# Memory keys of layer 0 as single fp32 products, memory norms kept for layer 1, and a scheduler with other durations

## The chip, the cores and the metric

One core of a Trainium2 chip runs the kernel. The time is device microseconds of one execution, the median of three runs: 822.15 us (821.66 to 822.86). TensorE (PE in the profile; its weight loads are PEld) multiplies, VectorE (DVE), ScalarE (ACT) and GpSimd (POOL) work element by element, SyncE (SP) issues all DMAs from one queue in order.

## What is computed

Two layers of a decoder trunk over 256 tokens of width 1024. Layer 0 mixes tokens by a gated delta rule (GDN), layer 1 by sparse attention (NSA). Both layers also attend to 256 memory tokens with 4 heads, and both normalise the same memory, each with its own weight vector:

```python
def rms_norm(x, w):
    y = x * lax.rsqrt(jnp.mean(x * x, axis=-1, keepdims=True) + EPS)
    return y * w

def memory_attention(qm, mem_n, w_kv):
    kv = (mem_n @ w_kv).reshape(B, -1, 2, MEM_HEADS, HEAD_DIM)
    k, v = kv[:, :, 0], kv[:, :, 1]
    s = jnp.einsum('bshd,bmhd->bhsm', qm, k) * HEAD_DIM ** -0.5
    return jnp.einsum('bhsm,bmhd->bshd', jax.nn.softmax(s, axis=-1), v)

for i in range(2):
    h = rms_norm(x, norm_mix_w[i])
    mem_n = rms_norm(mem, mem_norm_w[i])
    proj = h @ (gdn_w_in, nsa_w_in)[i]       # the last 512 columns are qm
    ...                                      # GDN or NSA on the other columns
    x = x + jnp.concatenate([mix, memory_attention(qm, mem_n, mem_w_kv[i])], -1) @ w_out[i]
    x = x + conv_glu(rms_norm(x, norm_ffn_w[i]), ffn_w_up[i], ...)
return rms_norm(x, final_norm_w)
```

The factor 1/rms of a memory token does not depend on the layer.

## The kernel before

**Products.** All matrices are cut into tiles of 128 by 128 weights against 128 by 256 data. The accuracy of fp32 is kept by splitting each operand into a high part and a rest in the type fp32r: `hi` is a rounded copy (ACT), `lo` is the difference (DVE, or POOL for memory weights). A product is then three fp32r products (`hi*hi`, `hi*lo`, `lo*hi`), in `proj`. Small products (scores, norms, GDN) are plain fp32 instead; the profile records one fp32 product as two matmul records. A weight chunk is loaded (`wr`, `mr`), cast (`wh`, `mh`) and subtracted (`wl`, `ml`) before TensorE uses it.

**The start.** `mem_in` makes `memh` and `meml` from the memory (`mt`) for values and keys, and squares it (`sq`, summed in `sqa`); `rstd_fin` sums the squares over partitions by products with `ones`, takes the power -1/2 on POOL (`rs`) and spreads the result over the partitions by products with the identity (`mx<-ident,rs`). `mem_k` makes one head's keys from 8 blocks of weights (24 products, tile `pf`) and scales them by the norm (`kTm`). The tokens `xall` go through the same norm, become `hn`, then `xh` and `xl`, and the projections `pj` of the GDN layer follow. For layer 1 `mem_in` loads the memory again, squares it by DVE or POOL (`sq_acc`) and takes the norm again.

**What sets the order.** Nothing runs in the order in which it is written. Class `Sched` (line 54) takes all operations, gives each a duration (`_cost`, line 416) and simulates the five engines: at each step the engine that can start earliest takes its next ready operation, buffers counted (`order`). What comes out is the fixed order of each engine's queue. For some operations it also chooses the engine (DVE or POOL). So a changed duration can move instructions anywhere. In the profile all of them carry the line of the helper that issues them, L379, and are told apart by tile names. In the change that line is L380.

**Durations in it.** An fp32r product of 256 columns counted 0.109 us, an fp32 one 0.43 us.

The lines that the change touches first:

```python
            if dt == F32R:
                return 0.0025 + max(2 * m, n) / 2400
            return 0.005 + 4 * max(m, n) / 2400
...
        for t in range(2):
            mm(pb[:, t * P:(t + 1) * P], rs[:, t:t + 1].to_broadcast([P, P]), ident, start=True, stop=True)
...
            xs.append(split(mts[k], V_NMEM + layer * KD + k, "mem", KD))
            if layer:
                acc = sq_acc(acc, mts[k])
            elif k % 2 == 0:
                acc = sq_pair(acc, mts[k].t)
        return (xs,) + rstd_fin(acc, keep="col")
```

Of the kernel before, what the change touches and what calls it, by code (L numbers as in the profile page):

```python
# [10 lines left out]
F32 = mybir.dt.float32  # L11
# [8 lines left out]
P = 128  # L20
# [35 lines left out]
class Sched:  # L56
# [66 lines left out]
    def order(self):  # L123
# [48 lines left out]
        while todo:  # L172
# [46 lines left out]
            if op.dma:  # L219
                hw_t = max(hw_t, st + 0.05) + 0.457  # L220
                dma_t = max(dma_t, hw_t + 0.65) + op.cost
                eng_t[op.eng] = st + 0.06
                op.end = dma_t + 0.75
            else:
                op.end = st + op.cost
                eng_t[op.eng] = op.end
            op.st = st
            out.append(op)
# [154 lines left out]
class Eng:  # L383
# [36 lines left out]
    def _cost(self, m, a, kw, out, e):  # L420
        ins = [x for x in list(a) + list(kw.values()) if isinstance(x, (Vt, Ap)) and x is not out]
        n = max([math.prod(x.shape[1:]) for x in [out] + ins[:2] if isinstance(x, (Vt, Ap))] or [1])
        ps = any((x.t if isinstance(x, Ap) else x).cls == "ps" for x in ins)
        if m == "dma_start":
            sh = out.shape
            return math.prod(sh) * 4 / 360e3
        if e == "tensor":
            n = math.prod(out.shape[1:])
            rhs = a[2]
            if m == "transpose":  # L430
                return 0.11
            dt = (rhs.t if isinstance(rhs, Ap) else rhs).dt
            m = out.shape[0]
            if dt == F32R:
                return 0.0025 + max(2 * m, n) / 2400
            return 0.005 + 4 * max(m, n) / 2400
        if e == "vector":
            if m == "reciprocal":
                return 0.06 + 0.0065 * n
            if m in ("tensor_copy", "tensor_scalar") and not ps:  # L440
                return 0.07 + 0.00055 * n
            return 0.07 + 0.00105 * n + (0.057 if m == "scalar_tensor_tensor" and isinstance(a[2], (Vt, Ap)) else 0.0)
        if e == "scalar":
            ex = sum(isinstance(kw.get(k), (Vt, Ap)) for k in ("bias", "scale")) + ("accum_out" in kw)
            if m == "mul" and isinstance(a[2], (Vt, Ap)):
                ex += 1
            return 0.075 + 0.00085 * n + 0.093 * ex
        if m == "scalar_tensor_tensor" or kw.get("op") == OP.pow and n > 8:
            return 1.0
        if kw.get("op") == OP.pow:  # L450
            return 0.3 + 0.165 * n
        if m == "tensor_scalar":
            return 0.08 + 0.0009 * n if not isinstance(a[2], (Vt, Ap)) else 0.26 + 0.0033 * n
        return 0.14 + 0.00215 * n
# [14 lines left out]
class Weights:  # L469
# [8 lines left out]
    def prep(self):  # L478
        c = self.next
        if c >= self.n:  # L480
            return
        self.next += 1
        sc, ch = self.cx, self.bpc * P
        w = min(ch, self.nblk * P - c * ch)
        raw = sc.tile(self.cls, [P, ch], F32, self.tag + "r", self.bufs)
        sc.t["sync"].dma_start(raw[:, :w], self.src[:, c * ch:c * ch + w])
        hi = sc.tile(self.cls, [P, ch], F32R, self.tag + "h", self.bufs)
        sc.t["scalar"].copy(hi[:, :w], raw[:, :w])
        lo = sc.tile(self.cls, [P, ch], F32R, self.tag + "l", self.bufs)
# [16 lines left out]
def body(ctx, tc, xT, memT, vecs, consts, rows, relb, w_few, w_in0, w_out0, w_up0, w_dn0, w_in1, w_out1, w_up1, w_dn1,  # L506
# [37 lines left out]
    def mx():  # L544
        return sc.tile("ps", [P, 512], F32, "mx", 6)
# [7 lines left out]
    def mm(*a, **kw):  # L553
        PE.matmul(*a, **kw)
# [74 lines left out]
    def sq_pair(acc, src, **kw):  # L629
# [5 lines left out]
            EV.tensor_tensor(out=nacc, in0=nacc, in1=acc, op=OP.add)  # L635
        return nacc

    def rstd_fin(*accs, keep="row"):
        pc = mx()
        for t in range(2):  # L640
            for i, acc in enumerate(accs):
                mm(pc[:, t:t + 1], acc[:, t * P:(t + 1) * P], ones[:, :1], start=i == 0, stop=i == len(accs) - 1)
        ms = Sm("ms", [P, 2])
        V.tensor_scalar(ms, pc[:, :2], 1.0 / D, EPS, op0=OP.mult, op1=OP.add)
        rs = Sm("rs2", [P, 2], 4)
        rsq(rs, ms, 2)
        pb = mx()
        for t in range(2):
            mm(pb[:, t * P:(t + 1) * P], rs[:, t:t + 1].to_broadcast([P, P]), ident, start=True, stop=True)
        if keep == "psum":  # L650
            return pb
        r = K("rs", 2)
        A.copy(r, pb[:, :S])
        return {"row": r, "both": (r, pb), "col": (r, rs)}[keep]
# [19 lines left out]
    def mem_load(k):  # L674
        mt = Dd("mt", 4)
        SY.dma_start(mt, memT[:, k * S:(k + 2) * S])
        return [mt[:, :S], mt[:, S:]]

    def mem_in(layer, mts):
        xs, acc = [], None  # L680
        for k in range(KD):
            xs.append(split(mts[k], V_NMEM + layer * KD + k, "mem", KD))
            if layer:
                acc = sq_acc(acc, mts[k])
            elif k % 2 == 0:
                acc = sq_pair(acc, mts[k].t)
        return (xs,) + rstd_fin(acc, keep="col")

    def mem_k(layer, h, ws, xs, rm):
        ps = proj(ws, h * KD, xs, "pf")  # L690
        kTm[layer, h] = K("kTm", 2 * MH)
        evac(ps, rm, kTm[layer, h])
# [90 lines left out]
        SY.dma_start(xall[:, k:k + 2], xT[:, k * S:(k + 2) * S].rearrange("p (k t) -> p k t", k=2), also_out=x[k:k + 2])  # L783

    wm0 = Weights(sc, w_mem0, 64, "m", 3, ahead=1, cls="d")
    mts = []
    xk = 0
    for ch in "wmmimmwxxxxsb0v":
        if ch == "m":
            mts += mem_load(len(mts))  # L790
        elif ch == "w":
            wm0.prep()
        elif ch == "x":
            x_load(xk)
            xk += 2
        elif ch == "i":
            ident = fixed([P, P], "ident")
            SY.dma_start(ident, consts[:, C_ID:C_ID + P])
        elif ch == "s":
            ms0 = mem_in(0, mts)  # L800
            mem_k(0, 0, wm0, *ms0[:2])
        elif ch == "b":
            wba = few_weights(w_few[:, :16 * KD], 16, "wba")
        elif ch == "0":
            w0.prep()
        elif ch == "v":
            vecb = fixed([P, NV - V_GNORM], "vecb")
            cst = fixed([P, C_HOT - C_TRI], "cst")
            SY.dma_start(cst, consts[:, C_TRI:C_HOT])
            SY.dma_start(vecb, vecs[:, V_GNORM:])  # L810
# [310 lines left out]
    classes["scl"] = classes["scd"] = 2  # L1121
    classes["gsc"] = 1
    pools["scl"] = pools["scd"] = pools["gsc"] = pools["dram"]
    for h in range(1, MH):
        mem_k(0, h, wm0, *ms0[:2])
    prs = [gdn_pair(p) for p in range(H // 2)]
    dh = 0
# [362 lines left out]
```

## Time and profile before

| what | value |
|---|---|
| median of three runs | 822.15 us |
| the profiled execution, its own time | 824.31 us |
| its span | 822.5 us |
| PE busy | 799.3 us (97%), 6645 records |
| DVE busy | 603.2 us (73%) |
| ACT busy | 480.1 us (58%) |
| POOL busy | 169.1 us (21%) |

A busy share is an average over stages. The first 230 us (memory, GDN) are different from the rest, where TensorE runs long lists of equal products. A matmul's duration overlaps the next one's, so the rate is read from the distance between starts. "What ended the idle time" names the last thing waited for.

### The profile page before, as it was taken

What the parts mean: (1) busy time and instruction counts of PE and PEld (TensorE: products, weight loads), DVE (VectorE), ACT (ScalarE), POOL (GpSimd) and SP (SyncE); (2) the same over time, 40 slices, a digit from 0 to 9 for tenths busy, and PEclk for the clock granted to TensorE, in tenths of its full rate; (3) what the DMA queues carried; (4) which work ended last, traced back from release to release, by engine and by line L of the source; (5) the groups of instructions that cost most, each with busy time, mean ns of one, the idle gap of its engine ahead of it and who ended that gap; (6) DMA issues with size and microseconds to landing.
All of it is one profiled execution on the core that took longest, in us unless ns stands there. A gap on an engine that the chain in (4) does not pass through costs nothing.

```text
span 822.5 us, 17100 instructions
## 1 busy us (share of the span) xinstructions
PE 799.3 (97%) x6645; PEld 784.5 (95%) x6645; DVE 603.2 (73%) x1243; ACT 480.1 (58%) x995; POOL 169.1 (21%) x273
## 2 busy tenths in 40 slices
PE   6999899999999999999999999999999999999996
PEld 5999889999999999999999999999999999999995
DVE  6999888887757576776765686798686867776552
ACT  6578475667644655555543466699845555664340
POOL 3267544544110211211101020000010211121000
PEclk9999999999999999999999999999999999999998
DMA  8674435443467456656666558522365656666641
GB/s 316 209 242 142 128 112 159 113 118 110 126 208 217 144 170 190 184 176 185 184 196 183 177 158 291 150 90 67 95 201 157 205 173 177 194 180 179 195 133 52
DMA packets 52926, 137.55 MB, mean 167 GB/s; under 512 B 11572, under 2 KB 17773, under 8 KB 52717
## 3 DMA queue, kind: packets, MB, share of 16 engines
q1 hardware_dynamic: 52844, 136.46, 54.8%
q8 instruction: 52, 0.85, 0.4%
q14 instruction: 30, 0.24, 0.1%
HBM read 134.06 MB, written 3.95 MB: 168 GB/s over the span
## 4 chain that ended last, share of the span: by engine, by line
PE 84%; DVE 5%; POOL 5%; DMA 3%; issue 2%; ACT 0%; SPq 0%; POOLq 0%; DVEq 0%
PE pj L379 69%; PE mx L379 11%; PE pf L379 4%; POOL DD L379 1%; DVE wl L379 1%; DMA cd<-scd 1%; POOL tm L379 1%; POOL sqa L379 1%; DVE DD L379 1%; DVE win L379 1%; DMA ident<-in_consts 1%; DMA scd<-DD 1%; DMA Lb<-scl 0%; POOL rs L379 0%; DVE cy L379 0%
## 5 line engine op out<-in xcount | busy, mean ns | idle before, releaser
L379 PE MATMUL pj<-xh,wh 128*128 128x256 f32 x1152 | 333.0, 289 | 0.0
L379 PE MATMUL pj<-xh,wl 128*128 128x256 f32 x1152 | 325.9, 283 | 1.1 <-DVE wl L379 1.1
L379 PE MATMUL pj<-xl,wh 128*128 128x256 f32 x1152 | 325.7, 283 | 0.0
L379 DVE TENSOR_TENSOR wl<-wr,wh 128x1024 fp32r<-128x1024 f32 x224 | 275.4, 1235 | 41.2 <-ACT wh L379 39.5
L379 ACT CAST wh<-wr 128x1024 fp32r<-128x1024 f32 x224 | 232.3, 1042 | 37.4 <-DVE wl L379 24.0
L379 PEld LDWEIGHTS pj<-xh,wl 128*128 128x128 f32 x1152 | 220.5, 191 | 1.5 <-DVE wl L379 1.3
L379 PEld LDWEIGHTS pj<-xh,wh 128*128 128x128 f32 x1152 | 220.7, 192 | 0.7
L379 PEld LDWEIGHTS pj<-xl,wh 128*128 128x128 f32 x1152 | 220.8, 192 | 0.2
L379 PE MATMUL pj<-gh,wh 128*128 128x256 f32 x352 | 99.6, 283 | 0.0
L379 PE MATMUL pj<-gl,wh 128*128 128x256 f32 x352 | 99.6, 283 | 0.0
L379 PE MATMUL pj<-gh,wl 128*128 128x256 f32 x352 | 99.6, 283 | 0.0
L379 POOL TENSOR_TENSOR fs<-fs,rs 128x256 f32<-128x256 f32 x44 | 39.2, 892 | 217.2 <-ACT fs L379 209.0
L379 PEld LDWEIGHTS pj<-gh,wh 128*128 128x128 f32 x352 | 67.6, 192 | 0.0
L379 PEld LDWEIGHTS pj<-gl,wh 128*128 128x128 f32 x352 | 67.6, 192 | 0.0
L379 PEld LDWEIGHTS pj<-gh,wl 128*128 128x128 f32 x352 | 67.6, 192 | 0.0
L379 PE MATMUL pj<-mixh,wh 128*128 128x256 f32 x192 | 55.2, 288 | 0.0
L379 PE MATMUL pj<-mixh,wl 128*128 128x256 f32 x192 | 54.3, 283 | 0.0
L379 PE MATMUL pj<-mixl,wh 128*128 128x256 f32 x192 | 54.3, 283 | 0.0
L379 DVE TENSOR_TENSOR fgr<-pj,rs 128x256 f32<-128x256 f32 x44 | 18.6, 423 | 46.2 <-PE pj L379 43.1
L379 DVE SCALAR_TENSOR_TENSOR fy<-fgr,vecb,fy 128x255 f32<-128x255 f32 x88 | 42.4, 482 | 10.8 <-ACT fy L379 10.3
L379 POOL TENSOR_TENSOR sq<-xall 128x256 f32<-128x256 f32 x6 | 9.0, 1506 | 200.6 <-DVE xall L379 200.6
L379 ACT ACTIVATE fs<-fy 128x256 f32<-128x256 f32 x44 | 18.4, 418 | 54.1 <-DVE fy L379 53.6
(314 smaller groups left out, 1410.2 us busy)
## 6 DMA issues: line engine op xcount, KB each, us to landing
wr<-in_w_up SPq DMA_DIRECT2D x88, 512.0 KB, 4.0
wr<-in_w_in SPq DMA_DIRECT2D x60, 512.0 KB, 4.3
wr<-in_w_dn SPq DMA_DIRECT2D x44, 512.0 KB, 3.7
wr<-in_w_out SPq DMA_DIRECT2D x24, 512.0 KB, 3.8
mr<-in_w_mem SPq DMA_DIRECT2D x32, 256.0 KB, 3.9
wr<-in_cw SPq DMA_DIRECT2D x8, 512.0 KB, 4.5
mt<-in_memT SPq DMA_DIRECT2D x8, 256.0 KB, 6.0
sk<-skr SPq DMA_DIRECT2D x1, 1536.0 KB
```

Of the source, the lines that this page charges most:

```text
L379: i = getattr(getattr(nc, self.eng), m)(*[fix(x) for x in a], **{k: fix(v) for k, v in kw.items()})
```

## The change

Five edits. (1) The keys of layer 0 are made by 8 fp32 products per head from the weights as loaded (`mr`) and the memory times the norm weight (`memf`); the cast and the subtraction of these weights go. The split memory is still made, for the values. (2) Ten fp32 products of `ones` with itself, whose result nobody reads, are put at the start of TensorE's queue. (3) The memory norm is copied by POOL into tiles that stay (`rmall`, `rcall`), and layer 1 uses it; its squares, sums and norm go. (4) In every norm the spreading by products with the identity becomes two transposes (`as_rows`). (5) The scheduler's durations of TensorE are others. A function `squares` is defined and called nowhere.

```diff
+    WARM, COLD = 6.0, 1.9
...
-                op.end = st + op.cost
+                op.end = st + op.cost * (self.COLD if op.eng == "tensor" and st < self.WARM else 1.0)
...
             if dt == F32R:
-                return 0.0025 + max(2 * m, n) / 2400
-            return 0.005 + 4 * max(m, n) / 2400
+                return max(0.013 + 2 * m / 2400, 0.01 + n / 2290)
+            return (0.009 if m > 32 else -0.028) + 4 * max(m, n) / 2400
...
+    def as_rows(rs):
+        pb = mx()
+        for t in range(2):
+            PE.transpose(pb[:, t * P:(t + 1) * P], rs[:, t:t + 1].to_broadcast([P, P]), ident)
+        return pb
...
+            if layer == 0 and N32:
+                full.append(K("memf", KD))
+                A.mul(full[k], mts[k], w)
+            if layer == 0 and k % 2 == 0:
+                acc = [sq_pair(acc[0] if acc else None, mts[k].t)]
         for k in range(KD):
             xs.append(split(mts[k], V_NMEM + layer * KD + k, "mem", KD))
-            if layer:
-                acc = sq_acc(acc, mts[k])
-            elif k % 2 == 0:
-                acc = sq_pair(acc, mts[k].t)
-        return (xs,) + rstd_fin(acc, keep="col")
+        if layer:
+            return xs
+        rm, rc = rstd_fin(*acc, keep="col")
+        rm_all = fixed([P, S], "rmall")
+        PO.tensor_copy(rm_all, rm)
+        rc_all = fixed([P, 2], "rcall")
+        PO.tensor_copy(rc_all, rc)
+        return xs, rm_all, rc_all, full
+
+    def mem_k32(h, ws, full, rm):
+
+        ps = pj("pf")
+        for k in range(KD):
+            mm(ps, ws.raw_block(h * KD + k), full[k], start=k == 0, stop=k == KD - 1)
+        kTm[0, h] = K("kTm", 2 * MH)
+        evac(ps, rm, kTm[0, h])
...
+    busy = mx()
+    for i in range(10):
+        op = PE.matmul(busy[:, :P], ones, ones, start=True, stop=True)
+        op.prio = 60
...
-        mem_k(1, h, wm1, *ms1[:2])
-    mem_v(1, wm1, ms1[0], ms1[2])
+        mem_k(1, h, wm1, ms1, ms0[1])
+    mem_v(1, wm1, ms1, ms0[2])
```

How the queues stand now, at three places. First the start of TensorE's queue. Before:

```order
1 L379 MATMUL pf_117<-memh_104,mh_99 128x256
2 L379 MATMUL pf_117<-meml_108,mh_99 128x256
3 L379 MATMUL pf_117<-memh_104,ml_102 128x256
4 L379 MATMUL pf_117<-memh_111,mh_99 128x256
5 L379 MATMUL pf_117<-meml_125,mh_99 128x256
6 L379 MATMUL pf_117<-memh_111,ml_102 128x256
```

Now:

```order
1 L380 MATMUL mx_90<-ones_78 128x128 x10
2 L380 MATMUL pf_116<-memf_110,mr_82 128x256
3 L380 MATMUL pf_116<-memf_121,mr_82 128x256
4 L380 MATMUL pf_116<-memf_125,mr_82 128x256
5 L380 MATMUL pf_116<-memf_133,mr_82 128x256
6 L380 MATMUL pf_116<-memf_138,mr_102 128x256
```

Ten products that need nothing but `ones` stand ahead, and each block of a key is one product instead of three.

Second, ACT's queue from the last square of the memory to the first cast of a GDN weight (`wh`); `sq<-xall` are the squares of the tokens. Before:

```order
14 L379 ACTIVATE sq_43_172<-mt_94 128x512
15 L379 ACTIVATE memh_181<-mt_94,vec_80 128x256
16 L379 ACTIVATE sq_64_190<-xall 128x512
17 L379 ACTIVATE sq_66_201<-xall 128x512
18 L379 ACTIVATE sq_68_209<-xall 128x512
19 L379 CAST mh_219<-mr_131 128x512
20 L379 CAST wba_226<-wbar_147 128x8x16
21 L379 ACTIVATE sq_70_228<-xall 128x512
22 L379 CAST wh_234<-wr_151 128x1024
```

Now:

```order
12 L380 ACTIVATE sq_33_159<-mt_98 128x512
13 L380 ACTIVATE memf_162<-mt_98,vec_80 128x256
14 L380 ACTIVATE memh_166<-mt_84,vec_80 128x256
15 L380 ACTIVATE memh_172<-mt_84,vec_80 128x256
...
21 L380 ACTIVATE memh_213<-mt_98,vec_80 128x256
22 L380 CAST wba_218<-wbar_140 128x8x16
23 L380 ACTIVATE sq_80_220<-xall 128x512
24 L380 ACTIVATE sq_82_225<-xall 128x512
25 L380 CAST wh_236<-wr_153 128x1024
26 L380 ACTIVATE sq_84_250<-xall 128x512
```

All eight `memh` now stand between the memory's squares and the tokens' squares.

Third, DVE's queue in the first GDN pair (`cy` is the convolution of a projection, `kT` the keys). Before:

```order
104 L379 SCALAR_TENSOR_TENSOR cy_808<-pj_807,vecb_186,cy_808 128x254
105 L379 TENSOR_TENSOR sq_952<-mt_841 128x256
106 L379 SCALAR_TENSOR_TENSOR cy_808<-pj_807,vecb_186,cy_808 128x253
107 L379 SCALAR_TENSOR_TENSOR cy_875<-pj_874,vecb_186,cy_875 128x255
108 L379 TENSOR_TENSOR sq_980<-mt_841 128x256
109 L379 SCALAR_TENSOR_TENSOR cy_875<-pj_874,vecb_186,cy_875 128x254
110 L379 SCALAR_TENSOR_TENSOR kT_994<-ct_978,cy_808 128x256
```

Now:

```order
98 L380 SCALAR_TENSOR_TENSOR cy_738<-pj_737,vecb_197,cy_738 128x254
99 L380 SCALAR_TENSOR_TENSOR cy_738<-pj_737,vecb_197,cy_738 128x253
100 L380 TENSOR_TENSOR wl_874<-wr_599,wh_851 128x1024
101 L380 SCALAR_TENSOR_TENSOR kT_898<-ct_867,cy_738 128x256
102 L380 SCALAR_TENSOR_TENSOR cy_800<-pj_799,vecb_197,cy_800 128x255
```

The squares of layer 1's memory are gone from between the convolutions.

## Rows read from the trace of the kernel before

**Rows 1.** The page's busy times: us, share of the span, number of instructions.

```profile
PE 799.3 (97%) x6645; PEld 784.5 (95%) x6645; DVE 603.2 (73%) x1243; ACT 480.1 (58%) x995; POOL 169.1 (21%) x273
```

**Rows 2.** The page's chain that ended last, by engine.

```profile
PE 84%; DVE 5%; POOL 5%; DMA 3%; issue 2%; ACT 0%; SPq 0%; POOLq 0%; DVEq 0%
```

**Rows 3.** Busy time in stretches of the span (stretch, its length, busy us of each engine with its instructions, granted TensorE clock, DMA share, GB/s).

```profile
20.00:22.00 2.00, 1.81 (x9) 1.59 (x8) 1.62 (x4) 1.12 (x2) 0.35 (x1) 1.00 1.03 405
50.00:75.00 25.00, 23.94 (x200) 23.61 (x199) 23.37 (x55) 21.96 (x57) 19.58 (x37) 1.00 0.67 218
75.00:100.00 25.00, 21.86 (x178) 20.90 (x177) 22.14 (x45) 13.76 (x27) 15.57 (x29) 1.00 0.50 150
100.00:200.00 100.00, 98.71 (x927) 93.46 (x928) 82.68 (x223) 64.63 (x171) 50.12 (x118) 1.00 0.41 116
```

**Rows 4.** TensorE in order of time: start, us from start to end, operation, idle before it and what ended that.

```profile
5.97 0.58 PE L379 MATMUL pf<-memh,mh 128*128 128x256 f32 x1 [5.97 <-ACT memh L379]
...
17.67 1.05 PE L379 MATMUL mx<-ident,rs 128*128 128x128 f32 x4
18.52 0.85 PE L379 MATMUL mx<-ones,sqa 128*128 128x1 f32 x4
...
20.41 1.22 PE L379 MATMUL mx<-ident,rs 128*128 128x128 f32 x4 [0.18 <-POOL rs L379]
...
23.77 0.41 PE L379 MATMUL pf<-memh,ml 128*128 128x256 f32 x1
23.99 0.41 PE L379 MATMUL pf<-memh,mh 128*128 128x256 f32 x1
...
24.52 0.28 PE L379 MATMUL pf<-memh,mh 128*128 128x256 f32 x1
...
25.60 0.28 PE L379 MATMUL pj<-xh,wba 128*32 128x256 f32 x1
...
41.12 0.28 PE L379 MATMUL pf<-mh,memh 128*128 128x256 f32 x1
```

**Rows 5.** TensorE in order of time, later: four fp32 products of 256 columns (8 records), eight transposes, the next product.

```profile
231.06 1.89 PE L379 MATMUL mx<-mpT,vm 128*128 128x256 f32 x8
232.79 1.04 PE L379 MATMUL mx<-ident,mp 128*128 128x128 f32 x8
233.58 0.36 PE L379 MATMUL pj<-mixh,wh 128*128 128x256 f32 x1
```

**Rows 6.** ACT in order of time at the start.

```profile
5.41 0.51 ACT L379 ACTIVATE memh<-mt,vec 128x256 fp32r<-128x256 f32 x1 [0.60 <-DMA mt<-in_memT]
5.82 0.61 ACT L379 ACTIVATE sq<-mt 128x512 f32<-128x512 f32 x1
6.34 0.49 ACT L379 ACTIVATE memh<-mt,vec 128x256 fp32r<-128x256 f32 x1
...
13.94 0.63 ACT L379 ACTIVATE sq<-xall 128x512 f32<-128x512 f32 x1
14.55 1.04 ACT L379 CAST wh<-wr 128x1024 fp32r<-128x1024 f32 x1
```

**Rows 7.** DVE in order of time at the start.

```profile
21.67 1.66 DVE L379 SCALAR_TENSOR_TENSOR hn<-xall,vec,mx 128x256 f32<-128x256 f32 x4 [0.38 <-PE mx L379]
23.24 1.09 DVE L379 TENSOR_TENSOR xl<-hn,xh 128x256 fp32r<-128x256 f32 x3
...
36.09 1.22 DVE L379 TENSOR_TENSOR wl<-wr,wh 128x1024 fp32r<-128x1024 f32 x1
```

**Rows 8.** POOL in order of time at the start.

```profile
10.53 2.64 POOL L379 TENSOR_TENSOR sqa<-sqa,sqa 128x256 f32<-128x256 f32 x1 [10.09 <-DVE sqa L379]
13.40 0.81 POOL L379 TENSOR_TENSOR sqa<-sq 128x256 f32<-128x256 f32 x1 [0.24 <-ACT sq L379]
...
19.65 0.70 POOL L379 TENSOR_TENSOR rs<-ms,nhalf 128x2 f32<-128x2 f32 x1 [2.39 <-DVE ms L379]
```

**Rows 9.** The norm of layer 1's memory: its squares on DVE (a tile's instructions: number, shortest, middle and longest ns, first and last start), the last sum on POOL, then TensorE in order of time around its products.

```profile
L379 DVE TENSOR_TENSOR sq<-mt x8: 413/416/959, 58.4 to 66.8; 128x256 f32<-128x256 f32 x8
...
71.11 1.71 POOL L379 TENSOR_TENSOR sqa<-sqa,sq 128x256 f32<-128x256 f32 x1
...
71.53 0.28 PE L379 MATMUL pj<-xh,wl 128*128 128x256 f32 x1
72.87 0.61 PE L379 MATMUL mx<-ones,sqa 128*128 128x1 f32 x4 [1.06 <-POOL sqa L379]
73.34 0.36 PE L379 MATMUL pj<-xh,wh 128*128 128x256 f32 x1
...
165.48 0.60 PE L379 MATMUL mx<-ident,rs 128*128 128x128 f32 x4
165.84 0.36 PE L379 MATMUL pf<-memh,mh 128*128 128x256 f32 x1
```

**Rows 10.** What TensorE waited for from 26 to 240 us: total us, times, longest.

```profile
PE mx L379 <- DVE kT L379: 1.6, 3, 1.0
PE pj L379 <- DVE wl L379: 1.1, 1, 1.1
```

**Rows 11.** The end of the program: TensorE and DVE in order of time.

```profile
815.69 0.71 PE L379 MATMUL mx<-ident,rs 128*128 128x128 f32 x4 [1.03 <-POOL rs L379]
...
816.44 0.69 DVE L379 TENSOR_TENSOR fin<-fin,mx 128x512 f32<-128x512 f32 x1 [1.58 <-PE mx L379]
```

More of the change, by code (lines that the diff above doesn't have):

```diff
@@ L492, in prep, with raw_block @@
         self.ready[c] = (hi, lo)
+    def raw_block(self, b):
+        c, r = divmod(b, self.bpc)
+        if c not in self.ready:
+            ch = self.bpc * P
+            raw = self.cx.tile(self.cls, [P, ch], F32, self.tag + "r", self.bufs)
+            self.cx.t["sync"].dma_start(raw, self.src[:, c * ch:(c + 1) * ch])
+            self.ready[c] = raw
+            self.next = max(self.next, c + 1)
+        return self.ready[c][:, r * P:(r + 1) * P]
     def block(self, b, n=1):
@@ L636, in sq_pair, with squares @@
         return nacc
+    def squares(src, **kw):
+        sq = Dd("sq0", 4, (P, 2, S))
+        A.activation(sq, src.rearrange("p (a b) -> p a b", a=2) if len(src.shape) == 2 else src, AF.Square, **kw)
+        return [sq[:, 0], sq[:, 1]]
+    def as_rows(rs):
[3 more added lines that the diff above has]
+        return pb
     def rstd_fin(*accs, keep="row"):
@@ L646, in rstd_fin @@
         rsq(rs, ms, 2)
-        pb = mx()
-        for t in range(2):
-            mm(pb[:, t * P:(t + 1) * P], rs[:, t:t + 1].to_broadcast([P, P]), ident, start=True, stop=True)
+        pb = as_rows(rs)
         if keep == "psum":
@@ L677, in mem_load @@
         return [mt[:, :S], mt[:, S:]]
+    N32 = 4
     def mem_in(layer, mts):
-        xs, acc = [], None
+        xs, acc, full = [], [], []
+        for k in range(KD):
+            w = vec[:, V_NMEM + layer * KD + k:V_NMEM + layer * KD + k + 1]
+            if layer == 0 and N32:
[3 more added lines that the diff above has]
+                acc = [sq_pair(acc[0] if acc else None, mts[k].t)]
         for k in range(KD):
             xs.append(split(mts[k], V_NMEM + layer * KD + k, "mem", KD))
-            if layer:
-                acc = sq_acc(acc, mts[k])
-            elif k % 2 == 0:
-                acc = sq_pair(acc, mts[k].t)
-        return (xs,) + rstd_fin(acc, keep="col")
+        if layer:
[8 more added lines that the diff above has]
+        ps = pj("pf")
+        for k in range(KD):
+            mm(ps, ws.raw_block(h * KD + k), full[k], start=k == 0, stop=k == KD - 1)
+        kTm[0, h] = K("kTm", 2 * MH)
+        evac(ps, rm, kTm[0, h])
     def mem_k(layer, h, ws, xs, rm):
@@ L791, in body @@
         elif ch == "w":
-            wm0.prep()
+            if N32:
+                wm0.raw_block(wm0.next * wm0.bpc)
+            else:
+                wm0.prep()
         elif ch == "x":
@@ L800, in body @@
             ms0 = mem_in(0, mts)
-            mem_k(0, 0, wm0, *ms0[:2])
+            for h in range(N32):
+                mem_k32(h, wm0, ms0[3], ms0[1])
+            if not N32:
+                mem_k(0, 0, wm0, *ms0[:2])
         elif ch == "b":
@@ L1123, in body @@
     pools["scl"] = pools["scd"] = pools["gsc"] = pools["dram"]
-    for h in range(1, MH):
+    for h in range(max(1, N32), MH):
         mem_k(0, h, wm0, *ms0[:2])
```

## The prediction

> **What bounds the kernel now.** I read the busy times first: TensorE is busy 97% of the span, DVE 73% [rows 1], and the chain that ended last lies on TensorE for 84% [rows 2]. So whatever does not shorten TensorE's queue, or its waits, is worth nothing. The table by stretches tells where it waits: 1.1 us from 50 to 75, 3.1 us from 75 to 100, 1.3 us from 100 to 200 [rows 3]. From 50 to 100 DVE is busy 23.4 and 22.1 of 25 us, so there it is a second bound. The order in time shows the start: TensorE begins at 5.97 us and its starts lie 0.22 us apart until about 24.2 us, then 0.12 us (nine products from 24.52 to 25.60) [rows 4]. For 256 columns that is the 1.2 GHz level, then the 2.4 GHz level. The granted clock reads 1.00 from 20 to 22 us [rows 3]; here only the distances show the level. It rose after TensorE had worked without a gap from 20.41 us. The earlier runs of products, broken by waits, did not raise it.
>
> **The change part by part.**
>
> *The start.* Ten products of `ones` cost nothing in place: TensorE idles until 5.97 us [rows 4]. At the low level an fp32 product of 128 columns takes 0.43 us (two from 17.67 to 18.52 [rows 4]), so they fill 4.3 us, from about 1.1 to 5.4 us. That is longer than the 3.8 us without a gap from 20.41 us, so I expect the high level from about 6 us.
>
> A key block costs one fp32 product, 0.43 us (four from 231.06 to 232.79 [rows 5]), in place of three at 0.12, 0.36 us. The 32 blocks take 13.8 us in place of 11.5 at the high level. That is 2.3 us more TensorE work, but it stands before 24 us, where the DMAs set the pace: they are full at 405 GB/s [rows 3], and by the sizes in SP's queue (7.0 MB up to and with the last key weights) these land at about 22 us. So keys end near 23.6 us. Today 36 key products stand behind the first token product at 25.60 us: 36 x 0.12 = 4.3 us. This is the most that the start can give.
>
> The tokens' norm sets what comes next, and it gets later. ACT now makes 8 `memf`, 4 squares and 8 `memh` before it squares the tokens. By the distance of starts, 0.41 us for one such and 0.52 us for a square [rows 6]: 5.41 + 16 x 0.41 + 8 x 0.52 + 1.0 (`wh`) + 0.9 (small copies, waits) = about 18.1 us, where the last square ends at 14.57 today [rows 6]. Today 7.1 us pass from there to `hn` at 21.67 [rows 7]. Now DVE and POOL have less between: adds of 0.4 and 0.8, the power 0.70 [rows 8], three `kTm`, two `wl` of 1.2 us [rows 7]: 4.6 to 6.4 us, `hn` at 22.7 to 24.5. Then DVE needs 8 x (0.41 + 0.36) us for `hn` and `xl` [rows 7] and 1.1 for a `kTm` and an `ml`, so `xl` is complete at 30.0 to 31.8. TensorE ends 64 products on it 2 us later, then 9 value products, a wait for the fourth `wl` (together 2.2 us, as its `wh` stands behind `ba`), and 24 more (2.9 us): 37.1 to 39.1 us. Today the same work ends at 41.12 + 9 x 0.12 = 42.2 us [rows 4]. That is 3.1 to 5.1 us, above what the 4.3 allows, and DVE's queue, the second bound, gains little. I take **3.0 us**, from below nothing (the clock rival) to 4.3.
>
> *Layer 1's memory norm.* Two products with `ones` (0.47 us to the next start, 72.87 to 73.34) and two with the identity (0.36 us, 165.48 to 165.84) go: 0.83 us. With the first goes a wait: 71.53 to 72.87 is 1.34 us in place of 0.12, since POOL's last sum runs from 71.11 to 72.82 [rows 9]. Together **2.0 us**. DVE also loses 8 squares of 0.42 us, from 58.4 to 66.8 [rows 9], and four sums of 0.41: 4.9 us just ahead of the stretch where TensorE idles 3.1 us, with `kT` and `wl` as what it waits for [rows 10]. That relief is worth 0 to 3.1 us. The waits also include some that come through POOL and the DMAs, so I take **1.5 us**.
>
> *Transposes.* Six norms stay, 12 products with the identity become 12 transposes. A product costs 0.18 us (0.36 for two [rows 9]), a transpose 0.10 us (eight from 232.79 to 233.58 [rows 5]): 12 x 0.08 = 1.0 us. The last norm is in nobody's shadow: 0.71 us to its end [rows 11] becomes about 0.4; beyond the 0.16 already counted that is 0.2 us. **1.2 us**. The Trainium skill (TensorE: Matmul & The Clock Gate, Terms) calls the transpose mode 4 times faster for fp32; by that estimate a transpose takes 0.045 us and the term is 1.8 us. The rows show 1.8 times, so they decide.
>
> *Order and durations.* With fp32r products at 0.12 us (0.122 in the code, 0.109 before) the scheduler's clock agrees with the trace, and GDN's queues are re-ordered throughout. What it may gain is the idle time left from 75 to 200 us, 4.4 us [rows 3] less the 1.5 already taken; what it may lose is at least another stretch like 75 to 100, 3.1 us. I take **0**, with 3 us to either side.
>
> Costs at nothing: the two norm copies on POOL (21% busy, hidden while TensorE has weights to wait for; without that cover they delay `hn` by 1 to 2 us), and the shorter ACT and DVE work on key weights before 25 us.
>
> **Sum:** 3.0 + 2.0 + 1.5 + 1.2 = 7.7 us. The profiled execution took 824.31 us, so 816.6 for it; it lay 2.2 us above the median of 822.15, from which I count: **814.4 us**. The forecast's own range is 811 to 818.
>
> **Rivals.**
>
> *The clock stays low after the ten products.* For: broken runs did not raise it, and the first head's products wait for `memf`. Then eight products of a head take 6.8 us and heads 1 and 2 run at that rate from 13 us until the level rises near 20 us as today; the start gives 0. 814.4 + 3.0 = 817.4 us. Against: the ten are longer than today's gapless 3.8 us.
>
> *POOL delays the tokens' norm.* An add on POOL took 2.64 us beside busy DVE at 10.53 us, 0.81 at 13.40 [rows 8]. Two adds and the copy of `rmall` at the long price put `hn` about 4 us later, and TensorE has no keys left to fill with: 818.4 us. The Trainium skill (GPSIMD Engine Reference, 1. Specifications) says POOL shares its SBUF interfaces with VectorE and contends with instructions of two SBUF inputs, such as `wl`; by that rule, to which the two rows agree, this delay comes, but only when `wl` falls on the adds.
>
> *A better order.* The agreeing clock removes the rest of the idle time to 200 us and some in NSA: 3 to 6 us more, 810 us.
>
> *DVE eats it.* TensorE leads but DVE does not, and each lead comes back as a wait for `wl`. Only the removed TensorE work counts, 0.8 + 1.0: 820.4 us, and 821 with any loss in the order.
>
> *Slower: the GDN inverses run dry.* In the new order `X`, `DX` products of 32 columns stand 16 in a row with no projection between. They depend on POOL and two DMAs. If each of the four 25 us stretches from 100 to 200 idled as 75 to 100 does, TensorE would lose 4 x 3.1 - 1.3 = 11.1 us: 814.4 + 11.1 = 825.5 us. It decides once these waits reach 9.4 us. For: DVE reaches the gates (`gg`) no earlier. Against: 4.9 us less DVE work just before.
>
> **Chances.** Forecast 0.58, low clock 0.13, POOL 0.08, better order 0.09, DVE 0.06, dry inverses 0.06. A measurement can tell about 0.2% (1.6 us) from no change: below 820.5 is faster. Faster 0.88, same 0.06, slower 0.06. The range 808.5 to 819.5 takes in the forecast, clock, POOL and most of the better order.
>
> **What would show it.** Right: product starts 0.12 us apart before 10 us; keys done near 24 us; `hn` after 22.7 us; the kT transposes 2 to 3 us before today's; no squares of `mt` near 60 us; TensorE idle from 75 to 100 below 2 us. Wrong: starts 0.22 us apart beyond 15 us, `hn` after 26 us, or more than 3 us idle in any stretch of 25 us from 100 to 200.

## The result: slower by 1.4%

The changed kernel takes 834.17 us (832.81 to 834.92, four runs) beside 822.5 us for the kernel before in the same comparison: a ratio of 1.0137 (95% interval 1.0114 to 1.0159), 11.7 us more. The forecast was 814.4 us, so it was wrong in sign. The profiled executions have spans of 832.3 and 822.5 us: 9.8 us to explain.

The busy times of the changed kernel, as in [rows 1]:

```profile
PE 800.3 (96%) x6613; PEld 782.1 (94%) x6613; DVE 601.1 (72%) x1226; ACT 477.4 (57%) x994; POOL 165.4 (20%) x267
```

TensorE idles 832.3 - 800.3 = 32.0 us, where it idled 822.5 - 799.3 = 23.2 [rows 1]. So 8.8 of the 9.8 us are waits. The table by stretches, with the columns of [rows 3], tells where:

```profile
50.00:75.00 25.00, 24.84 (x208) 24.65 (x207) 19.32 (x38) 23.28 (x61) 16.32 (x41) 1.00 0.79 243
75.00:100.00 25.00, 20.95 (x200) 19.97 (x198) 20.42 (x48) 12.13 (x27) 12.24 (x24) 0.86 0.40 116
...
125.00:150.00 25.00, 21.07 (x217) 19.80 (x217) 18.61 (x44) 13.02 (x30) 14.07 (x32) 1.00 0.44 123
100.00:200.00 100.00, 92.06 (x846) 88.14 (x843) 80.62 (x211) 63.05 (x161) 51.29 (x118) 1.00 0.42 115
```

From 50 to 75 us the change does what was forecast: the wait of 1.1 us is gone and DVE has 4 us less to do. From 75 to 100 TensorE idles 4.1 us (3.1 before), and from 100 to 200 it idles 7.9 us where it idled 1.3; 3.9 of them lie between 125 and 150. What it waits for there, as in [rows 10] (27 to 250 us):

```profile
PE mx L380 <- DVE kT L380: 4.2, 2, 4.0
PE mx L380 <- POOL DX L380: 2.2, 1, 2.2
PE mx L380 <- DVE o L380: 1.8, 3, 1.3
PE mx L380 <- DVE bv L380: 1.8, 1, 1.8
PE mx L380 <- ACT kT L380: 1.7, 1, 1.7
PE mx L380 <- DVE gg L380: 1.5, 1, 1.5
```

There is not one long wait but many, and these are the six groups with more than 1 us each. They are for work of three engines, all in the first 250 us. The longest, on TensorE in order of time:

```profile
75.75 0.28 PE L380 MATMUL pj<-xh,wl 128*128 128x256 f32 x1
80.07 0.69 PE L380 MATMUL mx<-ident,kT 128*128 128x128 f32 x2 [4.05 <-DVE kT L380]
...
82.91 0.41 PE L380 MATMUL pj<-xl,wh 128*128 128x256 f32 x1
83.12 0.41 PE L380 MATMUL pj<-xh,wl 128*128 128x256 f32 x1
...
85.10 0.29 PE L380 MATMUL pj<-xh,wh 128*128 128x256 f32 x1
85.22 0.28 PE L380 MATMUL pj<-xl,wh 128*128 128x256 f32 x1
```

Behind the wait the starts lie 0.21 us apart, then 0.12. The granted clock is 0.50 from 80 to 84 us and 1.00 from 85 to 90: the wait also cost the 2.4 GHz level until about 84.9 us. And DVE's queue in that time, where kT is made:

```profile
75.41 1.28 DVE L380 TENSOR_TENSOR DD<-DD,tm 32x63 f32<-32x63 f32 x1 [0.93 <-POOL tm L380]
76.62 0.46 DVE L380 SCALAR_TENSOR_TENSOR cy<-pj,vecb,cy 128x254 f32<-128x254 f32 x1
77.01 0.20 DVE L380 TENSOR_TENSOR tm<-Lb,DD 32x64 f32<-32x64 f32 x1
77.14 0.46 DVE L380 SCALAR_TENSOR_TENSOR cy<-pj,vecb,cy 128x253 f32<-128x253 f32 x1
77.54 0.68 DVE L380 TENSOR_TENSOR ml<-mr,mh 128x512 fp32r<-128x512 f32 x1
78.41 1.27 DVE L380 TENSOR_TENSOR DD<-DD,tm 32x63 f32<-32x63 f32 x1 [0.19 <-POOL tm L380]
79.61 0.41 DVE L380 SCALAR_TENSOR_TENSOR kT<-ct,cy 128x256 f32<-128x256 f32 x1
```

The last convolutions (`cy`) and `kT` stand behind steps of the inverse (`DD`, `tm`) that alternate between DVE and POOL. An in-order queue passes each wait for POOL on to whatever stands behind it.

### The profile page after: what moved, and what is told of

It is laid out like the page before. It is cut to its first block, busy times and chain, and to the rows that moved or that the text cites. A ratio compares the mean times of both kernels' runs of the same rounds, so it can differ in the third digit from the quotient of the medians.

```text
span 832.3 us, 17033 instructions
## 1 busy us (share of the span) xinstructions
PE 800.3 (96%) x6613; PEld 782.1 (94%) x6613; DVE 601.1 (72%) x1226; ACT 477.4 (57%) x994; POOL 165.4 (20%) x267
## 4 chain that ended last, share of the span: by engine, by line
PE 79%; POOL 6%; DVE 5%; DMA 4%; ACT 3%; issue 2%; POOLq 0%; SPq 0%; ACTq 0%
PE pj L380 65%; PE mx L380 11%; PE pf L380 3%; POOL DD L380 2%; POOL tm L380 1%; DVE wl L380 1%; ACT wh L380 1%; DMA cd<-scd 1%; DMA wr<-in_cw 1%; DVE DD L380 1%; POOL rs L380 1%; DMA mr<-in_w_mem 1%; DVE cy L380 1%; POOL g L380 1%; DMA Lb<-scl 1%
## 5 line engine op out<-in xcount | busy, mean ns | idle before, releaser
L380 POOL TENSOR_TENSOR fs<-fs,rs 128x256 f32<-128x256 f32 x44 | 47.8, 1087 | 217.7 <-ACT fs L380 217.7
L380 ACT CAST gh<-fg 128x256 fp32r<-128x256 f32 x44 | 17.9, 406 | 62.9 <-DVE fg L380 62.9
L380 DVE TENSOR_TENSOR fg<-fs,pj 128x256 f32<-128x256 f32 x44 | 18.5, 421 | 31.5 <-POOL fs L380 31.5
```

The lines of the kernel that those rows point to most:

```text
L380: i = getattr(getattr(nc, self.eng), m)(*[fix(x) for x in a], **{k: fix(v) for k, v in kw.items()})
```

## The experiments

All times are medians of several runs, the ratio is to the kernel before in the same comparison. "Idle" is the length of a stretch less PE's busy time in it.

| run | what is different | us | ratio, 95% interval | idle 27 to 125 | idle 125 to 250 |
|---|---|---|---|---|---|
| kernel before | | 822.5 to 824.6 | 1 | 5.1 | 0.8 |
| changed kernel | | 834.17 | 1.0114 to 1.0159 | 7.5 | 6.9 |
| e1 | changed, old durations | 820.84 | 0.9946 to 0.9973 | 4.4 | 2.5 |
| e2 | before, new durations | 840.38 | 1.0166 to 1.0222 | 8.4 | 6.4 |
| e3 | changed, no ten products | 834.39 | 1.0081 to 1.0172 | 8.6 | 6.4 |
| e4 | changed, split keys | 836.39 | 1.0112 to 1.0188 | 5.8 | 5.7 |
| e5 | changed, other engines longer | 827.77 | 1.0013 to 1.0043 | 8.3 | 2.4 |
| e6 | changed, fp32r old (0.109) | 821.86 | 0.9960 to 0.9985 | 3.7 | 3.0 |
| e7 | e1 with fp32r 0.098 | 826.08 | 1.0007 to 1.0034 | 7.9 | 1.2 |
| e8 | e1 with fp32r 0.136 | 878.51 | 1.0625 to 1.0683 | 7.4 | 10.6 |
| e9 | changed, 1.0 us to TensorE | 832.24 | 1.0077 to 1.0123 | 6.7 | 5.5 |
| e10 | changed, other engines longest | 824.99 | 0.9991 to 1.0024 | 5.7 | 1.2 |
| e11 | e1 with fp32r 0.112 | 833.83 | 1.0108 to 1.0139 | 7.1 | 7.5 |
| e12 | before, edits 3 and 4 | 827.48 | 1.0024 to 1.0054 | 7.4 | 3.3 |
| e13 | changed, kT ahead by hand | 834.24 | 1.0109 to 1.0145 | 7.5 | 6.6 |
| e14 | changed, ml on DVE | 834.94 | 1.0108 to 1.0151 | 6.8 | 6.9 |
| e15 | before with fp32r 0.110 | 827.3 | 1.0025 to 1.0051 | 5.7 | 2.2 |
| e16 | e1, ml on DVE | 821.84 | 0.9946 to 0.9979 | 3.7 | 3.5 |
| e17 | changed, layer 1's memory sooner | 838.65 | 1.0154 to 1.0184 | 7.6 | 7.2 |
| e18 | e1, layer 1's memory sooner | 826.61 | 1.0019 to 1.0060 | 6.7 | 4.2 |

**Which edit.** e1 puts the old durations back into the change, e2 puts the new ones alone into the kernel before:

```diff
-    WARM, COLD = 6.0, 1.9
+    WARM, COLD = 0.0, 1.9
-                return max(0.013 + 2 * m / 2400, 0.01 + n / 2290)
-            return (0.009 if m > 32 else -0.028) + 4 * max(m, n) / 2400
+                return 0.0025 + max(2 * m, n) / 2400
+            return 0.005 + 4 * max(m, n) / 2400
```

> The changed kernel with the scheduler's old durations; edits 1 to 4 stay. Theory O (the new durations order GDN's and NSA's queues so that TensorE waits, and the four other edits save what was forecast): about 822.5 - 5 = 817 us, 814 to 819, and less than 3 us of idle TensorE from 75 to 100. Rival F (the fp32 keys, done by 27 us, no longer fill TensorE's waits in the first GDN pairs, so the durations do not matter): 832 to 836 us, with some 4 us idle from 75 to 100 again. Rival L (any disturbance of the list scheduler moves the time by up to 10 us either way, and none of the edits is the cause by itself): anything from 812 to 835, with long waits at other places than in the changed kernel.

> The kernel before with the new durations alone. Theory O: slower, about 822.5 + 14 = 836 us (828 to 840), with waits of 2 us and more between 75 and 240. Rival F: no difference, 821 to 824 us. Rival L: anything from 815 to 835.

Theory O holds in both, in sign and nearly in size: each time is a little above its range, and e1 idles 3.7 us from 75 to 100, not less than 3. Rival L's range takes in e1 but not e2. The durations cost 834.17 - 820.84 = 13.3 us in the changed kernel (14.6 us by the two ratios, as the kernel before took 822.5 us in one comparison and 824.3 in the other) and 16 us in the kernel before. The other four edits save 824.31 - 820.84 = 3.5 us, not the 5 expected. Between the changed kernel and e1, idle falls from 32.0 to 22.0 us and busy time from 800.3 to 797.3:

```profile
PE 797.3 (97%) x6613; PEld 780.2 (95%) x6613; DVE 593.2 (72%) x1230; ACT 477.6 (58%) x994; POOL 162.7 (20%) x263
```

So of 13.0 us of span 10.0 are waits. The other 3.0 are the same products taking longer, as at 80.07.

e3 leaves out the ten products, e4 sets `N32 = 0`, which undoes edit 1.

> The changed kernel without the ten products of ones. The start's lead of 2.4 us at 40 us should go, since the clock then rises later: by theory O and by rival F 834 + 2 to 4 = 836 to 838 us. Rival L: the shifted first microseconds change the order of GDN too, so anything from 820 to 840.

> The changed kernel with layer 0's keys as split fp32r products again (edit 1 undone, edits 2 to 5 stay), so three heads' key products can fill waits after the start. Rival F: the waits of the first GDN pairs go, 818 to 824 us. Theory O: the durations still make the order, 830 to 838 us. Rival L: anything from 815 to 838.

e3 misses: nothing is lost. In its start the first token product comes 0.3 us later than in the changed kernel (27.12), not 2 to 4:

```profile
27.44 0.47 PE L380 MATMUL pj<-xh,wba 128*32 128x256 f32 x1
```

e4 falls on theory O's side: the keys as filler (rival F) do not undo the loss.

**Which duration, and how much.** e6 puts back the fp32r line alone; e7, e8 and e11 scale it in e1, e15 in the kernel before:

```diff
-                return 0.0025 + max(2 * m, n) / 2400
+                return 0.9 * (0.0025 + max(2 * m, n) / 2400)   # e7; e8: 1.25, e11: 1.03, e15: 1.01
```

> The changed kernel with the old duration of the fp32r products alone (0.109 us in place of 0.122); the new duration of the fp32 products and the slow first 6 us stay. Theory M: the fp32r products are 85 of 100 us of TensorE's plan, so nearly all of the loss goes: 819 to 824 us. If the fp32 durations or the slow start are the cause: 830 to 836 us. Rival L: anything from 812 to 838.

> The changed kernel with the old durations, and fp32r products shorter still: 0.098 us. Theory M: more margin yet, no waits that the changed kernel had, 816 to 822 us; at some point the plan runs TensorE dry and puts what is ready before what is urgent, which would cost. Rival L: anything from 812 to 838, no order by duration over 0.098, 0.109, 0.122 and 0.136.

> The changed kernel with the old durations, but fp32r products at 0.136 us, longer than they are on the chip (0.12). Theory M: less margin than in the changed kernel, so slower than its 834: 836 to 850 us. Rival R (the changed kernel's loss is an accident of its one order): 815 to 825 us as easily. Rival L: anything from 812 to 838.

> The changed kernel with the old durations, fp32r products 3% longer (0.112 us). It shows how far a small disturbance scatters the time. Theory M: between 0.109 (820.8 us) and 0.122 (about 834 us, or 822 with the old value alone put back), near 821 to 826 us. Rival L (the order is a lottery): over 5 us away from 820.8 either way as easily as not.

> The kernel before with fp32r products 1% longer in the plan (0.110 us in place of 0.109), nothing else. Theory L (the orders of GDN differ by luck, and a disturbance this small draws another): more than 3 us away from 824 either way, waits from 27 to 250 us of 7 to 15 us in place of 5.8. Rival M (only the ratio of the durations matters): 823 to 826 us.

e6 gives 821.86 us, so the fp32r duration is the cause; the fp32 one and the slow first 6 us are not. The scan is 826.1, 820.8, 833.8, 834.2 and 878.5 us at 0.098, 0.109, 0.112, 0.122 (the changed kernel) and 0.136. It rises from 0.109 on, but not smoothly: 3% already cost the whole 13 us, where theory M expected 0 to 5. Theory M misses at both ends too: e7 should have been no slower than 822 us, e8 no slower than 850. In e8 TensorE idles 51.8 us, where e1 has 22.0. There the loss spreads to the long lists of equal products and the weights themselves come too late, as its waits over the whole span show:

```profile
PE pj L380 <- DVE wl L380: 16.3, 28, 1.0
```

In the kernel before 1% costs about 3 us (827.3 beside 824.25), and the idle time from 27 to 250 us rises from 5.9 to 7.9. Theory L had named both, and theory M's range ends at 826. So differences of 3 us between two such kernels can come from the order alone, and no single edit can be credited with them.

**The ratio to the other engines.** By the code's formulas, summed over the plan, DVE takes 543 us, ACT 441 and POOL 118; the trace has 601, 477 and 165. TensorE took 721 in the plan with old durations and 793 with new, and 800 in the trace. e5 and e10 were made on the reading that the old durations were about a tenth short on all engines alike. They lengthen the others too; e9 adds margin in another way (`LAT`).

That reading goes wrong on DVE and ACT. Busy time runs to the end of each record, and records overlap. By the distance of starts, in the kernel before, DVE and then ACT:

```profile
36.09 1.22 DVE L379 TENSOR_TENSOR wl<-wr,wh 128x1024 fp32r<-128x1024 f32 x1
37.23 0.17 DVE L379 TENSOR_SCALAR e<-ee 128x16 f32<-128x16 f32 x1
```

```profile
48.65 1.04 ACT L379 CAST wh<-wr 128x1024 fp32r<-128x1024 f32 x1
49.59 0.40 ACT L379 ACTIVATE g<-g,ngc 128x128 f32<-128x128 f32 x1
```

A `wl` takes 1.14 us and a `wh` 0.94; the plan's formulas give 1.145 (0.07 + 0.00105 x 1024) and 0.945. Two neighbouring records overlap by 0.082 us on DVE, 0.097 on ACT and 0.040 on POOL (medians in the changed kernel). With this taken off each record, the trace has 557 us for DVE, 447 for ACT and 158 for POOL. So the plan is nearly right for DVE and ACT. Only POOL looks far short, and part of its time is waiting beside DVE, as the row at 23.63 below shows. e5 and e10 make DVE and ACT longer than they are.

```diff
+    OTHER = {"vector": 1.10, "scalar": 1.08, "gpsimd": 1.38}    # e5; e10: +0.075, +0.09, x1.35
...
-    LAT = {"tensor": 0.27, "vector": 0.17, "scalar": 0.2, "gpsimd": 0.18, "sync": 0.13}
+    LAT = {"tensor": 1.0, "vector": 0.17, "scalar": 0.2, "gpsimd": 0.18, "sync": 0.13}    # e9
```

> The changed kernel with new TensorE durations, and now the other engines' durations longer too: DVE by 1.10, ACT by 1.08, POOL by 1.38, the ratio of busy time in the trace to busy time in the plan. Theory M (margin: the old durations were short on all engines alike, by about a tenth; the change corrects TensorE alone, so the plan believes that DVE, ACT and POOL are quicker beside TensorE than they are, orders products just in time, and on the chip each comes too early): the ratio is restored, 816 to 823 us. Rival D (it is the longer TensorE duration itself, whatever the ratio): 830 to 836 us. Rival L (any disturbance scatters the time): anything from 812 to 838.

> The changed kernel with new TensorE durations; every DVE operation counts 0.075 us more, every ACT one 0.09 us, POOL's by 1.35, so the plan's busy times are 631, 523 and 171 us where the trace has 601, 477 and 165: the other engines are a little longer than they are. Theory M: as much margin as in the run with old durations, below the 827.8 us of the run with factors 1.10, 1.08 and 1.38: 816 to 824 us. Rival A: no order between them, 820 to 836 us.

> The changed kernel with all its new durations, and one more number: the plan hands a result to TensorE 1.0 us after it is done, in place of 0.27 us. Theory M (the loss is missing margin: with true TensorE durations the plan orders a product for the moment at which its operand is due, and on the chip that operand comes later): the margin is put back openly, 817 to 825 us. Rival A (the loss is an accident of the order, any order of true durations is as bad): 830 to 838 us.

e5 and e10 take back 6.4 and 9.2 of the 13.3 us. e5 is 4.8 us above theory M's range; e10 is 1.0 us above it and also lies in rival A's. e9 takes back 2 and misses. Margin as one number is not the remedy. But every order from a plan that holds TensorE long beside the others (0.112 us and more, the others as they were) is slow, and no other is. That is eight different orders (e13 and e14 keep the changed kernel's), so chance alone, as in theory L, is unlikely. The last column of the table parts the two groups: 5.5 us and more of idle from 125 to 250 in all runs of 832 us and above, 4.2 and less in all of 828 and below. The rows of that stretch for the kernel before, the changed kernel, e1 and e11:

```profile
125.00:250.00 125.00, 124.21 (x1118) 117.67 (x1117) 93.97 (x236) 76.27 (x194) 44.31 (x94) 1.00 0.49 146
```

```profile
125.00:250.00 125.00, 118.13 (x1070) 111.53 (x1070) 94.39 (x244) 76.23 (x193) 43.41 (x93) 1.00 0.46 136
```

```profile
125.00:250.00 125.00, 122.50 (x1104) 115.89 (x1104) 94.83 (x239) 75.51 (x191) 40.09 (x87) 1.00 0.48 149
```

```profile
125.00:250.00 125.00, 117.51 (x1033) 109.54 (x1033) 91.06 (x241) 73.21 (x193) 53.85 (x115) 0.99 0.41 121
```

DVE and ACT do about the same work in all four; TensorE fits 1118, 1070, 1104 and 1033 records in.

**Is one wait the loss?** e13 puts the last two convolutions, their activation and `kT` ahead of the `DD` at 75.41; e14 and e16 put POOL's `ml` on DVE. The rest of the order stays. (The `kT` is the third head's, not the second's as the expectation calls it.)

```diff
+        for i in (531, 532, 533, 534):          # e13: cy, cy, ct, kT ahead of DD
+            out.remove(by[i])
+            out.insert(out.index(by[448]), by[i])
...
+            if o.eng == "gpsimd" and "ml" in [t.tag for t in o.writes]:   # e14, e16
+                o.eng = "vector"
```

> The changed kernel with its own order, but four instructions put ahead by hand: the last two convolutions of the second GDN head's keys, their activation and the product that makes kT now stand in front of the step of the inverse (DD) that waits for POOL. All else keeps its place. Theory W (the named waits are the loss): TensorE's wait of 4.05 us at 75.75 us falls to about 1 us, the products behind it run at the 2.4 GHz level, and 2 to 4 us of it reach the end: 830 to 832 us. Rival B (another queue is the bound, and TensorE waits for it later instead): the wait goes and the end stays, 833.5 to 834.5 us.

> The changed kernel with its own order; the eight subtractions ml that the plan gave to POOL run on DVE at the same places of the order, not planned anew. At 75.41, 78.41 and 190.16 us a DVE operation of 0.2 us took 1.26 to 1.28 us and ended with POOL's ml that began 0.06 us before. Theory P (DVE is held up by POOL's ml): each of the three becomes 0.2 us, ml costs DVE 0.7 in its place, TensorE's waits at 75.75 and 190.17 shrink by 0.5 to 1 us each and 1 to 2 us reach the end: 832 to 833 us. Rival: DVE is the queue TensorE waits for, eight times 0.7 us more on it costs: 835 to 837 us.

> The changed kernel with the old durations (820.8 us), its own order, and the twelve ml of POOL on DVE as above. Theory P: 1 to 2 us less, 819 to 820 us, with the waits for ml (1.0 us at 78.68) and kT (2.0 at 92.1) shorter. Rival: DVE becomes later, 822 to 825 us.

e13 decides for rival B. On TensorE:

```profile
76.48 0.44 PE L384 MATMUL mx<-ident,kT 128*128 128x128 f32 x2 [0.62 <-DVE kT L384]
...
84.73 0.44 PE L384 MATMUL mx<-ident,vT 128*128 128x128 f32 x2 [3.39 <-DVE vT L384]
```

The wait of 4.05 us becomes 0.62, and 8 us later TensorE waits 3.39 us for the same head's `vT`: the sum is the same, and so is the end. In e14 the first `DD` falls from 1.28 us to

```profile
78.00 0.21 DVE L383 TENSOR_TENSOR DD<-DD,tm 32x63 f32<-32x63 f32 x1 [0.57 <-POOL tm L383]
```

and the wait for `kT` to 2.96 us, and the end does not move either: 834.94 us lies between the two ranges. e16 (821.84 us) cannot be told from e1 (820.84 us), as their runs overlap. It lies between its two theories and settles nothing.

**Is it a shortage of ready work?** From 75 to 150 us the changed kernel has 9 memory products (`pf`), e2 has 6 and e1 has 56. The count alone does not part slow from fast: the kernel before has 27, as e9 has, and e11 has 33. e17 and e18 give layer 1's memory a place sooner in the planner:

```diff
+    sc.off = -900        # e17; e18: -500, with old durations
     mts = []
     for k in range(0, KD, 2):
         mts += mem_load(k)
...
     mem_v(1, wm1, ms1, ms0[2])
+    sc.off = 0
```

> The changed kernel with all its durations; the operations of layer 1's memory (loads, splits, keys, values) stand 900 places sooner in the planner's priority, which brings about 39 memory products into its plan between 75 and 150 us in place of 9. Theory F2 (the waits are a shortage of ready work): 30 products x 0.12 = 3.6 us of the waits from 75 to 175 are filled and the rest of the memory work fills those to 250: 824 to 831 us. Rival S (any order at these durations is as bad; the extra casts and subtractions load DVE in a stretch where it is late already): 833 us or more.

> The changed kernel with the old durations (820.8 us), layer 1's memory 500 places sooner. Theory F2: the idle time of 5.5 us from 75 to 175 falls to 2 to 4 us and the last 51 memory products no longer stand behind the GDN layer: 817 to 820 us, faster than both kernels. Rival S: DVE is later still, 821 to 826 us.

Both times miss theory F2, but on the chip the edit did not bring the filler that F2 needs. From 75 to 150 us e17 ran 18 memory products, where 39 were planned, and e18 ran 54, no more than e1. In e17 the idle time from 75 to 175 drops from 10.1 to 7.2 us, but from 175 to 250 it rises from 2.6 to 5.3, of which 4.1 are for `ml`, and the end is 4.5 us later. So bringing filler sooner did not help, since it needs subtractions from queues that are late; whether a shortage of ready work is the cause is not shown.

**Edits 3 and 4 alone**, with old durations: e12.

> The kernel before with edits 3 and 4 alone (memory norms kept, transposes in place of products with the identity), old durations, split keys, no ten products. The forecast's terms for them are 2.0 + 1.5 + 1.2 = 4.7 us: 819 to 820 us beside a kernel before of 824. If the relief of DVE is worth nothing and the wait at 71.53 us comes back elsewhere, only the removed TensorE work is left, 0.8 + 1.2 = 2.0 us: 822 us. Rival L: 814 to 834 us.

All theories that named a gain miss. TensorE's busy time falls by 2.1 us (797.2 in place of 799.3), near the 2.0 forecast, but its idle time rises by 5.7.

## Why the prediction was wrong, point by point

**The step that failed is "Order and durations: 0, 3 us to either side".** Measured, it is a loss of 13 us in the changed kernel and 16 in the kernel before. The prediction reasoned that with 0.122 us "the scheduler's clock agrees with the trace". By the distance of starts that is so for TensorE, DVE and ACT, and not for POOL (118 us in the plan, 158 in the trace). What failed is the step from there to the order: that durations nearer to the trace cost nothing beyond 3 us. e6 shows that the one fp32r duration brings the loss. e5, e8 and e10 show that the loss follows its ratio to the other engines' durations, even where these are made longer than they are. Why this ratio makes bad orders stays open.

**The rival "the GDN inverses run dry" came nearest**, and its chance of 0.06 was far too small. It named the direction and the stretch and forecast 825.5 us. Its mechanism holds only in part: it named the `X` and `DX` products, but only 2.2 us of the waits above are for `DX`, and the longest are for `kT`. From 100 to 200 the idle time is 7.9 us of the 12.4 that it summed; the rest came before 100 us (`kT` 4.0, `gg` 1.5) and in NSA, where one wait of 0.6 us became 2.4:

```profile
493.94 0.35 PE L380 MATMUL mx<-wh,win 128*120 128x256 f32 x1 [2.38 <-DVE win L380]
```

It was also priced without the clock. What was said against it, 4.9 us less DVE work just before, did not help. The stated sign of error, more than 3 us idle in 25 us between 100 and 200, is the row 125 to 150 above.

**The start: 3.0 us.** The lead came in e1 but was gone by 47 us in the changed kernel, and part of the reason was wrong. (By its own terms the working ends at 38.9 us, not 39.1.)

```profile
1.05 4.64 PE L380 MATMUL mx<-ones 128*128 128x128 f32 x20 [1.05 <-DVE nhalf L380]
...
13.64 3.72 PE L380 MATMUL pf<-memf,mr 128*128 128x256 f32 x16 [0.73 <-DMA mr<-in_w_mem]
...
25.31 0.43 PE L380 MATMUL mx<-ident,rs 128*128 128x128 f32 x2 [0.34 <-POOL rs L380]
25.58 1.89 PE L380 MATMUL pf<-memf,mr 128*128 128x256 f32 x8
27.12 0.47 PE L380 MATMUL pj<-xh,wba 128*32 128x256 f32 x1
```

Sixteen records, eight key blocks, in 3.56 us are about the 0.43 us per block that was forecast, so the clock was high, and the rival of a low clock falls. But the last key products stand behind the tokens' norm in the queue. The keys end at 27.1 us, not 23.6, and by e3 the ten products bring 0.3 us there and nothing at the end. The tokens' `hn` is late as well, not 22.7 to 24.5 us:

```profile
25.78 1.26 DVE L380 SCALAR_TENSOR_TENSOR hn<-xall,vec,mx 128x256 f32<-128x256 f32 x3 [1.10 <-PE mx L380]
```

Part of this is the rival "POOL delays the tokens' norm": the power took 1.63 us, where it took 0.70 [rows 8], beside a `wl` on DVE from 23.47 to 24.69.

```profile
23.63 1.63 POOL L380 TENSOR_TENSOR rs<-ms,nhalf 128x2 f32<-128x2 f32 x1 [2.88 <-DVE ms L380]
```

The first `kT` transposes come at 42.96 us in e1, 4.5 before the 47.49 of the kernel before. In the changed kernel they come at 47.13.

**Layer 1's memory norm, 2.0 us, and the relief of DVE, 1.5.** The products and the wait at 71.53 [rows 9] are gone, and DVE is freed (19.3 us busy from 50 to 75, 23.4 in [rows 3]). The relief brought nothing that shows from 75 to 100: TensorE idles 4.1 us there (3.1 before), and under old durations 3.7 in e1 and 3.6 in e12, though 2.2 in e6.

**Transposes, 1.2 us.** The removed work is real: two products took 0.36 us [rows 9], two transposes take 0.13 (283.99 to 284.12 in the changed kernel). That is 0.11 us each, where 0.08 was forecast. At the end of the program, on TensorE and then on DVE,

```profile
825.44 0.60 PE L380 MATMUL mx<-ident,rs 128*128 128x128 f32 x2 [1.03 <-POOL rs L380]
```

```profile
826.08 0.69 DVE L380 TENSOR_TENSOR fin<-fin,mx 128x512 f32<-128x512 f32 x1 [1.47 <-PE mx L380]
```

`fin` starts 0.64 us after the transposes, where it was 0.75 [rows 11]: 0.1 us, not 0.2.

Together edits 1 to 4 bring 3.5 us (e1) in place of 7.7. That is inside the scatter that 1% and 3% of one duration showed, so how it divides among them stays open.

**What stays open.** Why the orders become bad between 0.110 and 0.112 us was not shown. It is no longer a question of one misplaced instruction (e13), of POOL's `ml` (e14) or of margin in the hand-over alone (e9). Two rivals are untested: POOL's duration set right by itself (e5 and e10 change three engines at once), and filler that does arrive before 150 us. e1 is the best version found: 820.84 us, 0.3 to 0.5% faster than the kernel before.

## What to carry to other kernels

A list scheduler orders by the ratios between its engines' durations, and a duration set nearer to the trace can make a worse order: try the old table under the new code first. Compare a planner's duration with the distance of starts, not with the length of a record or with busy time. Where many short chains cross several in-order queues, taking away the wait that the trace names only shows the next one; the idle time of the whole stretch is what must fall. Before a gain of 2 or 3 us is credited to an edit, see how far 1% on an unrelated duration moves the time.

## What the runs showed of the hardware

In the changed kernel each step of the inverse on DVE (`DD<-DD,tm`) that starts while POOL runs `ml` ends with it; there are three, at 75.41, 78.41 and 190.16 us. Beside the DVE rows at 75.41 and 78.41 above, POOL has

```profile
75.34 1.27 POOL L380 TENSOR_TENSOR ml<-mr,mh 128x512 fp32r<-128x512 f32 x1
...
78.35 1.26 POOL L380 TENSOR_TENSOR ml<-mr,mh 128x512 fp32r<-128x512 f32 x1
```

The ends are 76.61 and 76.69, then 79.61 and 79.68; without `ml` such a `DD` took 0.21 us (e14). The Trainium skill (Trainium Architecture — The Big Picture, What this means for kernel authors) says that VectorE and GpSimd share a port pair by an exclusive lock, not by a split of bandwidth; these rows agree. Not every DVE operation is held. In the kernel before, five that read TensorE's result (`mx`) ran at 0.25 us each beside an `ml` of POOL (210.90 to 212.17). In e1 an `ml` from 84.43 took 3.01 us itself, and a `DD` at 84.55 beside it took 0.17.

```profile
210.93 1.24 DVE L379 TENSOR_TENSOR DX<-DX,mx 32x64 f32<-32x64 f32 x5
```

After the wait of 4.05 us TensorE ran at 1.2 GHz from 80.07 to about 84.9 us. After a wait of 1.70 us it did not, as the same group of products tells:

```profile
132.44 0.44 PE L380 MATMUL mx<-ident,kT 128*128 128x128 f32 x2 [1.70 <-ACT kT L380]
...
133.75 0.36 PE L380 MATMUL pj<-xh,wh 128*128 128x256 f32 x1
```

It takes 1.31 us here and 2.48 (80.07 to 82.55) there. With nine products 0.21 us apart in place of 0.12 behind it, the lower level cost 2.0 us beside the wait's 4.05. In e13, after 3.39 us, the level fell only when TensorE had worked again for 1 us:

```profile
85.48 0.28 PE L384 MATMUL pj<-xl,wh 128*128 128x256 f32 x1
85.60 0.28 PE L384 MATMUL pj<-xh,wl 128*128 128x256 f32 x1
...
86.10 0.41 PE L384 MATMUL pj<-xh,wl 128*128 128x256 f32 x1
86.31 0.41 PE L384 MATMUL pj<-xh,wh 128*128 128x256 f32 x1
```

A wait of about 2 us cost the level in one run and not in another, at the same place of the same order. In the changed kernel TensorE waited 2.15 us for `DX` before 137.21; the granted clock stayed 1.00, and the products at 137.87 and 137.99 lie 0.12 us apart. In e13 it waited 2.05 us; the granted clock is 0.50 from 137 to 140 us:

```profile
136.50 0.81 PE L384 MATMUL mx<-DX,lm 128*128 128x128 f32 x4 [2.05 <-POOL DX L384]
...
137.32 0.41 PE L384 MATMUL pj<-xl,wh 128*128 128x256 f32 x1
137.54 0.41 PE L384 MATMUL pj<-xh,wl 128*128 128x256 f32 x1
```
